# Attention and state update of the sample tokens moved from the MLP's side work into the first state space branch

## The chip, the cores and the metric

The kernel runs on one core of a Trainium2 chip. The metric is the device time of one execution in microseconds (us), as the median of several runs. TensorE (PE in the profile) multiplies matrices into PSUM, VectorE (DVE) and ScalarE (ACT) do elementwise work, GpSimd (POOL) helps them, and SyncE (SP) issues most of the DMAs that move data between HBM and SBUF. Each engine works through its own list of instructions, in the order of the list.

## The reference

One step of a hybrid decoder layer. 2048 prompt tokens and 8 x 8 new tokens (the sample tokens, 8 sequences with a past of 8192 positions) go through one input projection; then, side by side, a dilated attention and a Mamba-2 state space branch; then one output projection, a squared-ReLU MLP of width 4096, and a norm. Everything is float32.

```python
def layer_prompt(h, lw):
    q, k, v, z, xbc, dt_raw = in_proj(h, jnp.arange(s), norm_mix, w_in)
    groups = [dilated_group_prompt(q, k, v, d, w // d) for (w, d) in DILATED_GROUPS]
    att = combine_groups(groups).reshape(b, s, D_ATT).astype(h.dtype)
    ssm, conv_state, ssm_state = ssm_branch(z, xbc, dt_raw, conv_prefix, h0, ...)
    h = out_and_mlp(h, att, ssm, w_out, norm_mlp, w_up, w_down)

def layer_sample(h, cache_k, cache_v, conv_prefix, h0, lw):
    k_ext = jnp.concatenate([cache_k.astype(k.dtype), k], axis=1)
    groups = [dilated_group_sample(q, k_ext, v_ext, d, w // d, n_past) for (w, d) in DILATED_GROUPS]
    att = combine_groups(groups).reshape(b, t, D_ATT).astype(h.dtype)
    ssm, conv_state, ssm_state = ssm_branch(z, xbc, dt_raw, conv_prefix, h0, ...)
    h = out_and_mlp(h, att, ssm, w_out, norm_mlp, w_up, w_down)
```

The two sample parts of this case are the attention of the new tokens over 1280 cached keys and values of each of the 8 sequences (`sample_att`), and their convolution and state update (`sample_ssm`). Their results are first needed by the output projection of the fourth and last tile of tokens.

## The kernel before

The work has three stages. First the input projection, then the prompt attention, in 16 steps of (key group, 512 tokens), with the rest of the input projection (tile `ps_xz`) woven in; then, tile by tile, output projection and MLP. A tile is 512 tokens, so there are four (T = 0 to 3); the sample tokens ride along with tile 3.

The state space branch of a tile (`branch`, with `ssd` for each of its four chunks of 128 tokens, and `merge`, which adds up the attention's parts) must be done before the tile's output projection `out`. The branch of tile 0 has nothing to hide behind but the end of the attention: the loop `for _ in branch(0, ...)` writes it out before `out(0)`. The branches of tiles 1 to 3 are side work of the MLP of the tile before: `work` yields after each small piece, and `tick`, called 64 times in a tile's MLP, draws as many pieces as the table `PLAN` says. In the kernel before, `work` also draws the sample parts: the state update ahead of the branch in the MLP of tile 0, the attention behind the branch in the MLP of tile 1.

Each multiplication in the projections is done three times, on high and low halves of the operands (`mm`, three matmuls of 512 columns a step); the weights are loaded as `raw_m` and split into `wm_h` (ScalarE) and `wm_l` (VectorE). The sample parts multiply float32 as it is, which TensorE does in two passes (the trace shows two matmuls for each one written). `sample_att` goes through pairs of sequences: keys (`kts`) times queries into `ps_ss`, with the mask added into `Sx` on VectorE; maximum, exponential, sum; eleven transposes into `ps_pt`, copied to `PT`; `PT` times values (`vts`) into `ps_po`; and two transposes into `ps_ao`. `sample_ssm` makes a convolution (`cv_s`), then for each of the 8 sequences loads a state `h0`, multiplies into `ps_yos` and `ps_sts` and adds the new state `hn_s`, and ends with a norm (`ps_sss`).

The order on each engine is set by a scheduler, which moves an instruction ahead of others where its own estimate of times says so, and by the pools: a tile that takes the place of an older one waits for the last use of that one. Pools stand on a left and a right stack. A hand-made dependency (`ld`, `behind`) keeps the first loads of the state update behind a certain load of output weights (`k.og`).

Of the kernel before, what the change touches and what calls it, by code (L numbers as in the profile page):

```python
# [9 lines left out]
F32 = mybir.dt.float32  # L10
# [7 lines left out]
P = 128  # L18
# [23 lines left out]
NBC = 2  # L42
# [8 lines left out]
NB2 = BS + max(SM)  # L51
WORK = ('', 'sb', 'ba', 'b')
LEAD = 4
# [11 lines left out]

PLAN = (plan((10, 10), (46, 48)), plan((38, 48), (18, 26)), plan((56, 48)))
OG = 3
# [39 lines left out]
def build(nc, tc, ctx, I, O, dbg=None, stop=None):  # L107
    dbg = dbg or {}
    k = K()
# [48 lines left out]
    pn = K()  # L158
# [672 lines left out]
    atx.close()  # L831
    te0 = p1x.enter_context(tc.tile_pool(name="te0", bufs=1, reuse_waits="tile", side="right"))
    tx0 = p1x.enter_context(tc.tile_pool(name="tx0", bufs=1, reuse_waits="tile", side="right"))
    if stop == "at":
        p1x.close()
        for nm, t in (("o12_s", o12_s), ("o3_s", o3_s), ("den_s", den_s), ("xzs_s", xzs_s)):
            if nm in dbg:
                nc.sync.dma_start(dbg[nm], t)
        return
# [38 lines left out]

    cx = ExitStack()
    tp = cx.enter_context(tc.tile_pool(name="dtp", bufs=1, reuse_waits="tile"))  # L880
    dent = tp.tile([P, P], F32, name="dent")
# [199 lines left out]
    def work(T, mix):  # L1081
        for part in WORK[T]:
            if part == "b":
                yield from branch(T, mix, pn)
            elif part == "s":
                yield from sample_ssm(nc, tc, I, O, psm, ident, ones, E)
            else:
                yield from sample_att(nc, tc, I, O, psm, ident, qs_s, ks_s, smx, kn_s)
        if SM[T]:
            mixsmp(T, mix)  # L1090

    def mm(ps, wh, wl, xh, xl, nk=4, first=True, last=True, after=None):
        for kk in range(nk):
# [7 lines left out]
    E = dict(dtv=dtv, ea_s=ea_s, nacum=nacum, wend=wend, decs=decs, bmask=bmask, convw=convw, convb=convb, dskip=dskip,  # L1101
             normw=normw, half_neg=half_neg, dr=dr, xzs_s=xzs_s, acs_s=acs_s, qs_s=qs_s, ks_s=ks_s, smx=smx, ld=lambda d: behind(d, k.og))
    for _ in branch(0, mix, nc, NBC, tx0, te0):
        pass
    wout0 = [load_wm(I["wout"][0, :, 4 * h:4 * h + 4]) for h in range(2)] if W0 else None
    cx.close()
    p1x.close()
    if stop == "smp":
# [221 lines left out]
def sample_ssm(nc, tc, I, O, psm, ident, ones, E):  # L1330
# [3 lines left out]
    NT = DB * DT  # L1334
    ld = E["ld"]
    with ExitStack() as cx:
        sp = cx.enter_context(tc.tile_pool(name="smp1", bufs=1, reuse_waits="tile"))
        mix = sp.tile([P, 4, NT], F32, name="mix")
# [110 lines left out]
def sample_att(nc, tc, I, O, psm, ident, qs_s, ks_s, smx, kn_s):  # L1449
    NT = DB * DT  # L1450
    with ExitStack() as cx:
        sp = cx.enter_context(tc.tile_pool(name="smp", bufs=1, reuse_waits="tile"))
        mix = sp.tile([P, 4, NT], F32, name="mixA")
# [25 lines left out]
        for bp in range(DB // 2):  # L1479
            Sx = sp.tile([P, NEWP + DT], F32, tag="Sx", name="Sx", bufs=1)  # L1480
            V = []
            for be in range(2):
# [5 lines left out]
                for n0 in range(0, NEWP + DT, 512):  # L1488
# [3 lines left out]
                    for pr in range(2):  # L1492
                        kt = sp.tile([P, 512], F32, tag="kts", name="kts", bufs=3)
                        nc.sync.dma_start(kt[:, :m1 - n0], I["kTs"][b][:, pr, n0:m1])
                        lq = qz[:, pr, b].rearrange("p e j t -> p (e j t)")
                        o = ps[r0 + 32 * pr:r0 + 32 * pr + 32]
                        nc.tensor.matmul(o[:, :m1 - n0], lq, kt[:, :m1 - n0], start=True, stop=True, skip_group_check=True)
                        if n1 > NEWP:
                            nc.tensor.matmul(o[:, m1 - n0:n1 - n0], lq, kn[:, pr, b * DT:(b + 1) * DT], start=True, stop=True,
                                             skip_group_check=True)  # L1500
# [24 lines left out]
            for be in range(2):  # L1525
                o = po[64 * be:64 * be + 64, :256]
                for j in range(5):
                    v = sp.tile([P, 2, 256], F32, tag="vts", name="vts", bufs=2)
                    nc.sync.dma_start(v, I["vTs"][2 * bp + be][:, 2 * j:2 * j + 2])
# [174 lines left out]
```

## Time and profile before

| | us |
|---|---|
| median of 3 runs | 2806.09 |
| lowest, highest | 2802.56, 2806.14 |
| the profiled execution, its own time | 2806.49 |
| its span in the trace | 2804.8 |

The page gives for each engine its busy time: TensorE 2627.4 us (94% of the span), VectorE 1718.9 (61%), ScalarE 1164.7 (42%), GpSimd 487.3 (17%). In the parts of a page and the answers of the trace, L1531 is line 1531 of the kernel, PE matmuls, PEld the weight loads before them; `ps_po<-vts,PT` is what an instruction writes and reads, by tile names. A matmul's record runs from its start until its result is there, over the start of the next one. The granted clock is a share of TensorE's full 2.4 GHz. Idle time of an engine carries the name of what ended it.

### The profile page before, as it was taken

The page shows a single profiled execution, that of the slowest core. Times are in us where ns is not written, and L with a number is a line of the kernel's source. Part 1 is how long each engine was busy: PE and PEld are TensorE (multiplying, and loading weights), DVE is VectorE, ACT ScalarE, POOL GpSimd, SP SyncE. Part 2 cuts the span into 40 slices and gives each one's busy share as a digit, 9 for nine tenths or more (in the row PEclk, how much of TensorE's full clock was granted, in tenths as well). Part 3 has the DMA queues.
Part 4 walks back from the last instruction along what each step waited for, and adds up shares of the span by engine and source line. Part 5 has one row for each costly group of instructions (what it writes and reads, how often), then busy time and mean ns, then how long its engine had stood idle before and what let it go on. Part 6 is the DMA issues. An engine that isn't in the chain of part 4 may idle for free.

```text
span 2804.8 us, 41924 instructions
## 1 busy us (share of the span) xinstructions
PE 2627.4 (94%) x15190; PEld 2274.1 (81%) x15190; DVE 1718.9 (61%) x2995; ACT 1164.7 (42%) x2243; POOL 487.3 (17%) x406
## 2 busy tenths in 40 slices
PE   7999699999854899999999999999999999999998
PEld 7999699899743677888888886666678889999998
DVE  6444277767797745777558775444477764555455
ACT  5333245454563424444454443233255344332333
POOL 2221044534443210010121010011010003000000
PEclk9999899999856899999999999999999999999999
DMA  7666687979344544454465445465455424533332
GB/s 253 205 208 186 176 256 198 262 221 261 115 125 142 182 152 154 147 165 134 153 210 169 148 141 174 135 200 176 156 177 165 152 100 158 174 101 105 104 102 83
DMA packets 341439, 464.30 MB, mean 166 GB/s; under 512 B 38096, under 2 KB 217488, under 8 KB 340192
## 3 DMA queue, kind: packets, MB, share of 16 engines
q1 hardware_dynamic: 314768, 437.96, 50.3%
q10 hardware_dynamic: 26464, 23.66, 2.6%
q8 instruction: 120, 1.97, 0.3%
q14 instruction: 87, 0.71, 0.1%
HBM read 366.12 MB, written 128.96 MB: 177 GB/s over the span
## 4 chain that ended last, share of the span: by engine, by line
PE 84%; DMA 6%; DVE 5%; SPq 2%; issue 2%; ACT 1%; POOL 1%; DVEq 0%; ACTq 0%; POOLq 0%
PE ps_dn L1094 9%; PE ps_dn L1096 9%; PE ps_up L1096 9%; PE ps_up L1094 9%; PE ps_dn L1097 9%; PE ps_up L1097 9%; PE ps_qk L600 3%; PE ps_o L1096 2%; PE ps_o L1094 2%; PE ps_o L1097 2%; PE ps_xz L180 2%; PE ps_xz L183 2%; PE ps_xz L184 2%; PE ps_po L1531 1%; PE ps_pv L724 1%
## 5 line engine op out<-in xcount | busy, mean ns | idle before, releaser
L873 ACT ACTIVATE wm_h<-raw_m 128x512 fp32r<-128x512 f32 x576 | 362.1, 630 | 838.0 <-PE ps_dn L1096 474.4
L874 DVE TENSOR_TENSOR wm_l<-raw_m,wm_h 128x512 fp32r<-128x512 f32 x576 | 416.5, 725 | 121.0 <-ACT wm_h L873 102.3
L1094 PE MATMUL ps_up<-xh_m,wm_h 128*128 128x512 f32 (+1 forms) x1280 | 458.6, 358 | 0.0
L1094 PE MATMUL ps_dn<-uh,wm_h 128*128 128x512 f32 (+1 forms) x1280 | 458.5, 359 | 0.0
L1096 PE MATMUL ps_dn<-ul,wm_h 128*128 128x512 f32 (+1 forms) x1280 | 457.1, 357 | 0.0
L1096 PE MATMUL ps_up<-xl_m,wm_h 128*128 128x512 f32 (+1 forms) x1280 | 456.9, 357 | 0.0
L1097 PE MATMUL ps_dn<-uh,wm_l 128*128 128x512 f32 (+1 forms) x1280 | 456.0, 357 | 0.0
L1097 PE MATMUL ps_up<-xh_m,wm_l 128*128 128x512 f32 (+1 forms) x1280 | 455.7, 356 | 0.0
L1207 DVE TENSOR_TENSOR acc<-acc,ps_dn 128x512 f32<-128x512 f32 (+1 forms) x320 | 189.4, 593 | 241.1 <-PE ps_dn L1097 238.0
L1094 PEld LDWEIGHTS ps_dn<-uh,wm_h 128*128 128x128 f32 x1280 | 240.3, 188 | 43.5 <-issue 11.0
L1096 PEld LDWEIGHTS ps_dn<-ul,wm_h 128*128 128x128 f32 x1280 | 240.3, 188 | 39.0 <-issue 6.5
L1096 PEld LDWEIGHTS ps_up<-xl_m,wm_h 128*128 128x128 f32 x1280 | 241.1, 188 | 37.1 <-issue 4.5
L1097 PEld LDWEIGHTS ps_dn<-uh,wm_l 128*128 128x128 f32 x1280 | 240.5, 188 | 37.6 <-issue 4.1
L1097 PEld LDWEIGHTS ps_up<-xh_m,wm_l 128*128 128x128 f32 x1280 | 241.4, 189 | 35.5 <-issue 2.0
L1094 PEld LDWEIGHTS ps_up<-xh_m,wm_h 128*128 128x128 f32 x1280 | 241.2, 188 | 34.5 <-issue 1.2
L1195 DVE SCALAR_TENSOR_TENSOR r<-ps_up,rs 128x512 f32<-128x512 f32 (+1 forms) x160 | 95.5, 597 | 141.7 <-PE ps_up L1097 140.5
L1198 DVE TENSOR_TENSOR ul<-r,uh 128x512 fp32r<-128x512 f32 (+1 forms) x160 | 96.7, 604 | 93.3 <-ACT uh L1197 93.3
L180 PE MATMUL ps_xz<-xq,wh 128*128 128x256 f32 (+1 forms) x512 | 146.6, 288 | 7.2 <-DMA xq<-xn_s 7.1
L183 PE MATMUL ps_xz<-xq,wh 128*128 128x256 f32 (+1 forms) x512 | 146.6, 287 | 0.0
L184 PE MATMUL ps_xz<-xq,wl 128*128 128x256 f32 (+1 forms) x512 | 145.8, 286 | 0.0
L600 PE MATMUL ps_qk<-qt,kA 128*128 128x256 f32 x300 | 103.5, 355 | 41.1 <-DMA qt<-q_s 35.1
L1196 ACT ACTIVATE r<-r 128x512 f32<-128x512 f32 (+1 forms) x160 | 88.8, 555 | 115.4 <-DVE r L1195 114.6
(355 smaller groups left out, 5273.6 us busy)
## 6 DMA issues: line engine op xcount, KB each, us to landing
raw_m<-wup SPq DMA_DIRECT2D x256, 256.0 KB
raw_m<-wdn SPq DMA_DIRECT2D x256, 256.0 KB
xq<-xn_s SPq DMA_DIRECT2D x48, 512.0 KB
am<-o_s SPq DMA_DIRECT2D x128, 128.0 KB
raw_m<-wout SPq DMA_DIRECT2D x64, 256.0 KB
ks<-ck SPq DMA_DIRECT2D x32, 510.0 KB
vs<-cv SPq DMA_DIRECT2D x32, 510.0 KB
xz_s<-ev SPq DMA_DIRECT2D x96, 128.0 KB
```

The costliest lines, as they stand in the source:

```text
L180: r = nc.tensor.matmul(ps, wh(kk), xh(kk), start=kk == 0, stop=False)
L183: nc.tensor.matmul(ps, wh(kk), xl(kk), start=False, stop=False)
L184: k.zl = nc.tensor.matmul(ps, wl(kk), xh(kk), start=False, stop=kk == KT - 1)
L600: k.mm = nc.tensor.matmul(ov, kt[:, ksl], mv, start=first, stop=False, skip_group_check=True)
L873: k.at["ACT"] = nc.scalar.activation(hi, raw, AF.Copy)
L874: nc.vector.tensor_tensor(lo, raw, hi.bitcast(F32), op=ALU.subtract)
L1094: behind(nc.tensor.matmul(ps, wh[:, kk], xh(kk), start=first and kk == 0, stop=False), after)
L1096: nc.tensor.matmul(ps, wh[:, kk], xl(kk), start=False, stop=False)
L1097: r = nc.tensor.matmul(ps, wl[:, kk], xh(kk), start=False, stop=last and kk == nk - 1)
L1195: nc.vector.scalar_tensor_tensor(r, ps, 0.0, c(X.rs), op0=ALU.max, op1=ALU.mult)
L1198: nc.vector.tensor_tensor(c(ul), r, c(uh).bitcast(F32), op=ALU.subtract)
L1207: k.at["DVE"] = nc.vector.tensor_tensor(h, h, ps, op=ALU.add)
```

## The change

The two sample parts leave `work` and become one generator, `samples()`: attention first, then state update. While the branch of tile 0 is written out, one piece of it is drawn after each piece of the branch, from the fourth on; what is left is drawn behind. `PLAN` becomes the same for three tiles: 48 pieces of a branch over 56 slots. The sample parts take their PSUM banks from the pool `pa` (three banks, as the projections do) instead of `pm`. Their SBUF pools stand on the right stack, in the place of the input projection's weights, whose pool now closes as soon as the attention is written out; the tiles of branch 0 (`te0`, `tx0`) move from the right stack to the left, in the place of the attention's tiles. The key loads get 6 buffers instead of 3, the value loads 4 instead of 2, and the dependency `ld` goes.

```diff
-WORK = ('', 'sb', 'ba', 'b')
+WORK = ('', 'b', 'b', 'b')
...
-PLAN = (plan((10, 10), (46, 48)), plan((38, 48), (18, 26)), plan((56, 48)))
+PLAN = (plan((56, 48)),) * 3
...
     atx.close()
-    te0 = p1x.enter_context(tc.tile_pool(name="te0", bufs=1, reuse_waits="tile", side="right"))
-    tx0 = p1x.enter_context(tc.tile_pool(name="tx0", bufs=1, reuse_waits="tile", side="right"))
+    p1x.close()
...
     cx = ExitStack()
+    te0 = cx.enter_context(tc.tile_pool(name="te0", bufs=1, reuse_waits="tile"))
+    tx0 = cx.enter_context(tc.tile_pool(name="tx0", bufs=1, reuse_waits="tile"))
...
         for part in WORK[T]:
-            if part == "b":
-                yield from branch(T, mix, pn)
-            elif part == "s":
-                yield from sample_ssm(nc, tc, I, O, psm, ident, ones, E)
-            else:
-                yield from sample_att(nc, tc, I, O, psm, ident, qs_s, ks_s, smx, kn_s)
+            yield from branch(T, mix, pn)
...
-    for _ in branch(0, mix, nc, NBC, tx0, te0):
+    def psp(name):
+        return pa.tile([P, 512], F32, tag="pa", name=name)
+
+    def samples():
+        yield from sample_att(nc, tc, I, O, psp, ident, qs_s, ks_s, smx, kn_s)
+        yield from sample_ssm(nc, tc, I, O, psp, ident, ones, E)
+
+    smp = samples()
+    for i, _ in enumerate(branch(0, mix, nc, NBC, tx0, te0)):
+        if i >= LEAD - 1:
+            next(smp, None)
+    for _ in smp:
         pass
     wout0 = [load_wm(I["wout"][0, :, 4 * h:4 * h + 4]) for h in range(2)] if W0 else None
     cx.close()
-    p1x.close()
...
-    ld = E["ld"]
+    ld = lambda d: d
...
-        sp = cx.enter_context(tc.tile_pool(name="smp1", bufs=1, reuse_waits="tile"))
+        sp = cx.enter_context(tc.tile_pool(name="smp1", bufs=1, reuse_waits="tile", side="right"))
...
-        sp = cx.enter_context(tc.tile_pool(name="smp", bufs=1, reuse_waits="tile"))
+        sp = cx.enter_context(tc.tile_pool(name="smp", bufs=1, reuse_waits="tile", side="right"))
...
-                        kt = sp.tile([P, 512], F32, tag="kts", name="kts", bufs=3)
+                        kt = sp.tile([P, 512], F32, tag="kts", name="kts", bufs=6)
...
-                    v = sp.tile([P, 2, 256], F32, tag="vts", name="vts", bufs=2)
+                    v = sp.tile([P, 2, 256], F32, tag="vts", name="vts", bufs=4)
```

What the scheduler makes of it is seen at three places. The first is VectorE's list in the last steps of the prompt attention (`S`, `M`, `den` and `lo` are the attention's tiles; `cv`, `xc` and `zt` are those of branch 0; `Sx` and `mixA` the sample attention's). Before:

```order
L672 TENSOR_TENSOR M<-S_6884,S_6909 128x1024
L930 SCALAR_TENSOR_TENSOR cv<-xc,convw,cv 128x128
L104 TENSOR_TENSOR lo<-S_6718,hi 128x512
L930 SCALAR_TENSOR_TENSOR cv<-xc,convw,cv 128x128 x2
L675 TENSOR_TENSOR M<-M,S_6265 128x2x256
L675 TENSOR_TENSOR M<-M,S_6266 128x2x256
L930 SCALAR_TENSOR_TENSOR cv<-xc,convw,cv 128x128 x8
L104 TENSOR_TENSOR lo<-S_6743,hi 128x512
```

And VectorE now, at the same place:

```order
L672 TENSOR_TENSOR M<-S_6884,S_6909 128x1024
L104 TENSOR_TENSOR lo<-S_6718,hi 128x512
L675 TENSOR_TENSOR M<-M,S_6265 128x2x256
L675 TENSOR_TENSOR M<-M,S_6266 128x2x256
L734 TENSOR_TENSOR den<-S_6265,S_6718 128x2x256
L734 TENSOR_TENSOR den<-S_6266,S_6718 128x2x256
L104 TENSOR_TENSOR lo<-S_6743,hi 128x512
L737 TENSOR_TENSOR den<-den,S_6743 128x1024
L104 TENSOR_TENSOR lo<-S_6743,hi 128x512
L1550 COPY mixA<-ps_ao 64x2x2x8 x4
L1507 TENSOR_TENSOR Sx<-ps_ss,sk 64x512 x2
```

The convolutions of the branch's first two chunks (48 instructions, L930) stood among the attention's and now stand behind all of it; in their place are the first two pairs of the sample attention.

The second place is SP's list where the loads of branch 0 begin (`xc`, `ar`, `zt`, `ea`). Before, among the loads of the last steps of the attention:

```order
L623 DMA V_6711<-v_s 128x4x128
L901 DMA xc<-xz_s 128x8x128
L627 DMA dV_6713<-v_s 128x4x128
L903 DMA ar<-ac_s 128x1024
L908 DMA zt<-xz_s 128x4x128
L912 DMA ea<-ac_s 64x4x128 x2
```

And SP now, behind the attention's last stores (`o_s`):

```order
L1500 DMA kts<-kTs 128x512 x4
L770 DMA o_s<-O_7191 1024x1x128
L884 DMA r_s<-dent 128x128
L1500 DMA kts<-kTs 128x256 x2
L770 DMA o_s<-O_7213 1024x1x128
L1500 DMA kts<-kTs 128x512 x4
L1500 DMA kts<-kTs 128x256 x2
L901 DMA xc<-xz_s 128x8x128
L903 DMA ar<-ac_s 128x1024
L908 DMA zt<-xz_s 128x4x128
```

The first load of the branch has moved behind the attention's end and behind two rounds of key loads, each round of which fills all six key buffers.

The third place is TensorE's list ahead of the first output projection (`ps_o`; `ps_ys` and `ps_sss` are the end of the state update). Before, it stood in the middle of branch 0:

```order
L1003 MATMUL ps_ss<-ones_r,sq_9389 128x1 x2
L947 MATMUL ps_xt<-ident,cv 128x128 x4
L955 MATMUL ps_bt<-ident,cv 128x128
L956 MATMUL ps_bt<-cv 128x128
L955 MATMUL ps_bt<-ident,cv 128x128
L956 MATMUL ps_bt<-cv 128x128
L1094 MATMUL ps_o<-mix_9265,wm_h 128x512
```

And TensorE now:

```order
L1407 MATMUL ps_yos<-h_10446,cm 64x256 x2
L1407 MATMUL ps_yos<-h_10463,cm 64x256 x2
L1426 MATMUL ps_ys<-ident,yo 128x64 x4
L1429 MATMUL ps_ys<-ar_s,xdt_s 64x64 x8
L1442 MATMUL ps_sss<-ones_r,sq_s 64x1 x2
L1089 MATMUL ps_o<-mix_9267,wm_h 128x512
```

The first output projection now stands behind all but the last matmul of the state update.

## Rows read from the trace of the kernel before

**Rows 1.** The page's second part: tenths of busy time and granted clock, 40 slices.

```profile
PE   7999699999854899999999999999999999999998
...
PEclk9999899999856899999999999999999999999999
```

**Rows 2.** Windows: stretch us, its length, busy us (instructions) by engine, clock, DMA share, GB/s.

```profile
core 0: us, PE busy (x) PEld busy (x) DVE busy (x) ACT busy (x) POOL busy (x), PEclk, DMA share, GB/s
735.00:840.00 105.00, 61.33 (x233) 48.09 (x233) 98.58 (x137) 63.83 (x122) 52.67 (x33) 0.61 0.44 126
840.00:934.00 94.00, 43.51 (x202) 31.23 (x201) 63.20 (x137) 32.40 (x72) 25.88 (x21) 0.64 0.39 120
...
1100.00:1690.00 590.00, 590.00 (x2734) 479.34 (x2733) 422.43 (x778) 274.08 (x520) 74.84 (x66) 1.00 0.50 161
1690.00:2060.00 370.00, 370.00 (x1552) 252.64 (x1552) 168.40 (x276) 121.89 (x211) 23.36 (x20) 1.00 0.53 168
2060.00:2600.00 540.00, 540.00 (x3295) 488.89 (x3294) 334.28 (x625) 223.74 (x429) 51.10 (x49) 1.00 0.43 139
```

**Rows 3.** Groups by line, TensorE, 1690 to 2060 us: x count, busy us, mean ns, idle.

```profile
L1531 PE MATMUL ps_po<-vts,PT 128*64 128x256 f32 x160 | 41.8, 390 | 0.0
...
L1497 PE MATMUL ps_ss<-kts,qz 128*32 128x512 f32 (+1 forms) x96 | 35.6, 532 | 0.0
...
L1472 PE MATMUL ps_kn<-ident,kn 128*64 128x128 f32 x2 | 0.4, 270 | 0.0
```

**Rows 4.** Groups by line, TensorE, 970 to 1100 us.

```profile
L1407 PE MATMUL ps_sts<-xw_s,bm 64*128 64x256 f32 x32 | 9.0, 402 | 0.0
L1401 PE MATMUL ps_yos<-h,cm 128*64 128x256 f32 x32 | 8.4, 389 | 0.0
...
L1436 PE MATMUL ps_sss<-ones_r,sq_s 128*64 128x1 f32 x4 | 0.4, 202 | 0.0
```

**Rows 5.** Chain of waits, 1690 to 2060 us, shares by line.

```profile
by line: PE ps_dn L1094 10.9%; PE ps_dn L1096 10.8%; PE ps_up L1096 10.7%; PE ps_po L1531 10.7%; PE ps_up L1097 10.6%; PE ps_up L1094 10.4%; PE ps_dn L1097 10.4%; PE ps_ss L1497 8.7%; PE ps_o L1096 4.3%; PE ps_o L1094 4.2%; PE ps_o L1097 4.
```

**Rows 6.** Groups by line, VectorE, 1690 to 2060 us.

```profile
L874 DVE TENSOR_TENSOR wm_l<-raw_m,wm_h 128x512 fp32r<-128x512 f32 x95 | 66.2, 698 | 42.4 <-ACT wm_h L873 39.0 <-ACT ao L1536 2.1 <-DMA h_s<-hst 1.0
...
L1501 DVE TENSOR_TENSOR Sx<-ps_ss,sk 64x512 f32<-64x512 f32 (+1 forms) x24 | 14.3, 602 | 26.3 <-PE ps_ss L1497 21.2 <-PE ps_ss L1499 5.1
...
L1456 DVE MEMSET qz<- 128x512 f32 x1 | 0.5, 485 | 0.1
```

**Rows 7.** Groups by line, VectorE, 930 to 1100 us.

```profile
L1353 DVE SCALAR_TENSOR_TENSOR cv_s<-xc_s,convw,cv_s 128x64 f32<-128x64 f32 x24 | 6.9, 348 | 0.0
...
L1437 DVE TENSOR_SCALAR rc_p<-ps_sss 64x2 f32<-64x2 f32 x1 | 0.2, 151 | 0.7 <-PE ps_sss L1436 0.7
```

**Rows 8.** Timeline, VectorE: start us, us, line, what, [idle before, releaser].

```profile
786.01 1.16 DVE L930 SCALAR_TENSOR_TENSOR cv<-xc,convw,cv 128x128 f32<-128x128 f32 x1
...
838.92 0.69 DVE L104 TENSOR_TENSOR lo<-S,hi 128x512 fp32r<-128x512 f32 x1 [0.44 <-ACT hi L103]
...
847.15 0.95 DVE L883 RECIPROCAL dent<-dent 128x128 f32<-128x128 f32 x1 [2.59 <-DMA dent<-den_s]
...
923.80 0.16 DVE L1004 TENSOR_SCALAR rc_s<-ps_ss 128x2 f32<-128x2 f32 x1 [3.90 <-PE ps_ss L1003]
...
928.59 0.69 DVE L104 TENSOR_TENSOR mix<-y,mix 128x512 fp32r<-128x512 f32 x1 [0.69 <-ACT mix L103]
...
934.31 0.69 DVE L1150 TENSOR_TENSOR hst<-hst,ps_o 128x512 f32<-128x512 f32 x1 [4.43 <-PE ps_o L1097]
```

**Rows 9.** Groups by line, VectorE, 735 to 934 us.

```profile
L104 DVE TENSOR_TENSOR lo<-S,hi 128x512 fp32r<-128x512 f32 x28 | 23.8, 859 | 5.0 <-ACT hi L103 5.0
```

**Rows 10.** DMA issues by line, 1690 to 2060 us: count, KB each.

```profile
vts<-vTs SPq DMA_DIRECT2D x40, 256.0 KB
...
kts<-kTs SPq DMA_DIRECT2D x32, 256.0 KB
...
kts<-kTs SPq DMA_DIRECT2D x16, 128.0 KB
```

More of the change, by code (lines that the diff above doesn't have):

```diff
@@ L1101, in build @@
     E = dict(dtv=dtv, ea_s=ea_s, nacum=nacum, wend=wend, decs=decs, bmask=bmask, convw=convw, convb=convb, dskip=dskip,
-             normw=normw, half_neg=half_neg, dr=dr, xzs_s=xzs_s, acs_s=acs_s, qs_s=qs_s, ks_s=ks_s, smx=smx, ld=lambda d: behind(d, k.og))
-    for _ in branch(0, mix, nc, NBC, tx0, te0):
+             normw=normw, half_neg=half_neg, dr=dr, xzs_s=xzs_s, acs_s=acs_s, qs_s=qs_s, ks_s=ks_s, smx=smx)
+    def psp(name):
[8 more added lines that the diff above has]
+    for _ in smp:
         pass
@@ L1106, in build @@
     cx.close()
-    p1x.close()
     if stop == "smp":
```

## The prediction

> **What bounds the kernel now.** I read the page's slices first: TensorE is at nine tenths from the fifteenth slice to the end, and dips before it, down to 4 and 5, where the granted clock dips too [rows 1]. The windows by stage say how deep. From 1100 to 2600 us TensorE is busy in every microsecond, at clock 1.00, whether sample work is there (1690 to 2060) or not (2060 to 2600) [rows 2]. So in the MLP a microsecond of TensorE is one of the program. From 735 to 934 us it is otherwise: TensorE is busy 61.33 + 43.51 = 104.8 of 199 us at a clock of 0.61 and 0.64, and VectorE 98.58 + 63.20 = 161.8. VectorE has hardly a gap in the first part, the attention's end (6.4 of 105 us), and 30.8 of 94 in the second, branch 0 alone [rows 2]. The timeline shows why: the convolutions of the branch start at 786, among the attention's work; the attention's last split is at 838.9; then VectorE waits in short steps for a store to come back (dent, 2.59 us) and for a chain through TensorE and GpSimd (rc_s, 3.90 us), until the last `mix` at 928.6 lets the first full output projection end at 934.3 [rows 8]. I call 735 to 934.3 us the stretch; VectorE bounds it first, the branch's chain second.
>
> **What leaves the MLP.** Sample attention on TensorE, seven groups from L1531 (160 matmuls, 41.8 us) and L1497 (96, 35.6 us) to L1472 (0.4 us), sums to 92.6 us [rows 3]. The state update, nine groups from L1407 (9.0) and L1401 (8.4) to L1436 (0.4), sums to 22.0 [rows 4]. These are lengths of records, which run over the start of the next. The chain gives L1531 and L1497 10.7% and 8.7% of 370 us, 71.8 us [rows 5], where the groups say 77.4: a factor 0.928. So (92.6 + 22.0) x 0.928 = 106 us of a full engine go. Nothing I see is late in their place: without sample work TensorE was still busy 540 of 540 us [rows 2]. The other side work of the MLP, three branches, stays.
>
> **What the stretch takes on.** VectorE: sample attention, seven groups from 14.3 (L1501) to 0.5 us (L1456), together 31.6 [rows 6]; state update, 19 groups from 6.9 (L1353) to 0.2 (L1437), together 25.7 [rows 7]. Sum 57.3, call it 58 with a few more weight splits that now stand ahead of the first `hst`. VectorE's list keeps all its other work, only in another order: before the attention's last split it loses two chunks of convolutions and gets two pairs of sequences, behind it the reverse and the rest. If VectorE's idle time stays as long as it was (37 us), the stretch grows by 58.
>
> Three things speak for more. First, branch 0 starts late: its first load stands behind two rounds of key loads, and the second round needs its six buffers back, that is, TensorE's products of the first round. While SP waits there, everything behind is late too: the branch's loads, the merge's, and the next values. Where VectorE before had convolved chunks to go on with, it has a few Sx rows. Second, the first part will hardly shrink by the convolutions it loses, since sample matmuls now sit between the attention's on TensorE and wait for keys. Third, the first output projection stands behind the end of the state update, a chain VectorE - TensorE - VectorE - ScalarE - VectorE - TensorE; before, 5.7 us lay between the last `mix` and the first `hst` [rows 8]. No row shows these waits. From below they are worth less than nothing: the sample work may fill gaps of VectorE, at most all 37 us [rows 2]. From above I bound them by the stretch's own worst: if each part had as much idle time again as the second part (30.8 us), +62. I take +15, near the 13 us that the two waits of 2.59 and 3.90 us make if each comes twice [rows 8]: about 7 for the first part, 8 for the ends of the second. So the stretch grows by 58 + 15 = 73.
>
> The other engines have room, if only just. DMA: 40 x 256 KB of values and 32 x 256 + 16 x 128 KB of keys are 20 MB [rows 10]; the stretch moved 126 and 120 GB/s at a share of 0.44 and 0.39 [rows 2], so about 290 GB/s at a full share, and 20 MB are some 70 us of the 115 us that are free in 199. The loads cost nothing in sum, though in the first part more than half of them meet the attention's own. TensorE: 106 us more at full clock beside 104.8 x 0.62 = 65 us makes 171 of 272.
>
> **Two rules against the change.** The same form of split, two SBUF inputs of 128x512, took 859 ns in the stretch [rows 9] and 698 in the MLP [rows 6], and GpSimd is busy 52.67 of 105 us there against 23.36 of 370 [rows 2]. The Trainium skill, GPSIMD Engine Reference, Specifications, says that GpSimd's way to SBUF is shared with VectorE and that the two contend when a VectorE instruction has two SBUF inputs; the trace agrees in kind. By that rule, and with the whole ratio of 1.23, the 58 us would be 71 and the time 13 us longer; I leave it in the range, since most sample instructions have one input in PSUM or one input alone.
>
> The other is the clock, and gives a rival: granted 1.00 where TensorE is always busy, 0.61 where it is busy for 58% [rows 2], which is a mix of its levels of 1.2 and 2.4 GHz. The Trainium skill, TensorE: Matmul & The Clock Gate, What's actually happening, says that the throttled state is the default and only activity releases it; the trace agrees. So the moved matmuls are dearer where they go unless they themselves keep the clock up.
>
> **The sum.** Against the profiled execution: 2806.5 - 106 + 73 = 2773.5, say 2774 us. Its own time is 0.4 us over the median of 2806.09, which changes nothing.
>
> **Rivals.**
> - *The gaps fill.* Sample pieces and branch pieces do not depend on each other, so one's waits are the other's work. For it: 30.8 us of idle time in branch 0 that come from one chain with nothing beside it [rows 2, 8]. Against it: lists are in order, and a sample instruction that waits for keys holds the branch. With half the 37 us filled, the stretch grows by 58 - 18 = 40: 2740 us.
> - *TensorE becomes the bound of the stretch (slower).* If the clock stays low, because TensorE keeps waiting for keys, values, splits and upper masks in turn, 106 us become 212 at 1.2 GHz; with the 104.8 us that are there, 317 us instead of 199, a growth of 118: 2806.5 - 106 + 118 = 2818. For it: the clock of 0.61 with matmuls spread over the whole stretch, and attention matmuls that now queue behind sample ones that wait for a load. Against it: slices next to the dip with TensorE at nine tenths have the full clock [rows 1]. It decides the sign once the stretch grows by more than 106.
> - *The MLP does not give it all back.* If the splits of weights (L874, 66.2 us in 370 [rows 6]) or their loads cannot follow a TensorE freed of side work, part of the 106 is lost; with a fifth lost, 2795. Against it: the 540 us without sample work [rows 2].
>
> **How the numbers follow.** Forecast 0.60, with 2756 to 2798 as its own range; gaps fill 0.17; TensorE bound 0.16; MLP keeps a part 0.07. A measurement of this kernel can tell about 0.2%, 5.6 us, from no change: faster means below 2800.5. The forecast is faster but for 0.03, the second all of it, of the third 0.13 slower and 0.03 the same, of the last half faster. So faster 0.77, same 0.09, slower 0.14. The range, 2738 to 2812, reaches to the gap-filling time, with GpSimd's contention and most of TensorE's rival at the other end.
>
> **What would show it.** In the profile after: no `ps_po`, `ps_sts` in the MLP, TensorE still without a gap there, and the MLP from the first `hst` to the end shorter by some 106 us; the first `hst` near 934 + 73 = 1007 us; the attention's last split between 838 and 850; VectorE busy about 220 us between 735 and that `hst`; the clock in the stretch well over 0.62. The prediction is wrong in the MLP if TensorE shows idle time there, and wrong in the stretch if the first `hst` is before 970 or behind 1040 us.

## The result, and the profile after

The changed kernel took 2770.36 us (median of 4 runs, 2763.89 to 2775.28), the kernel before, beside it on the same chip, 2804.32. The ratio is 0.988, with a 95% interval of 0.9855 to 0.9904: 1.2% faster. The prediction was 2774 us, with 2738 to 2812 as its range. The profiled execution after is the fastest of the four, 2763.89 us with a span of 2762.2.

The page's second part after, tenths of busy time of TensorE and its granted clock in 40 slices, which answers to [rows 1]:

```profile
PE   7999789999986689999999999999999999999998
...
PEclk9999889999998789999999999999999999999999
```

The dip is still there, two slices wide, but not so deep: 6 and 6 where it was 5 and 4, and the clock falls to 7 instead of 5. The windows of the changed kernel, with the columns of [rows 2]:

```profile
735.00:840.00 105.00, 90.21 (x440) 59.22 (x439) 89.78 (x123) 56.08 (x99) 48.62 (x31) 0.90 0.72 224
840.00:1009.50 169.50, 107.69 (x461) 65.71 (x461) 120.47 (x289) 59.41 (x140) 36.23 (x32) 0.75 0.60 172
1100.00:1690.00 590.00, 590.00 (x2689) 478.96 (x2688) 389.88 (x702) 258.11 (x479) 60.99 (x54) 1.00 0.49 155
1690.00:2060.00 370.00, 370.00 (x1676) 300.37 (x1675) 234.32 (x420) 164.69 (x301) 42.55 (x36) 1.00 0.50 158
2060.00:2560.00 500.00, 500.00 (x3111) 457.04 (x3110) 291.71 (x534) 199.31 (x377) 42.93 (x43) 1.00 0.41 132
```

In the MLP TensorE is again busy in every microsecond at clock 1.00, now without sample work. In the first part of the stretch it has gone from 61 to 90 us of 105, and the clock from 0.61 to 0.90: the moved matmuls keep it up themselves. VectorE's timeline of the changed kernel (start, length, line, what, idle before and its releaser), which answers to [rows 8]:

```profile
835.62 0.69 DVE L104 TENSOR_TENSOR lo<-S,hi 128x512 fp32r<-128x512 f32 x1 [1.57 <-ACT hi L103]
...
843.16 0.69 DVE L1507 TENSOR_TENSOR Sx<-ps_ss,sk 64x512 f32<-64x512 f32 x1 [3.30 <-PE ps_ss L1503]
...
855.18 5.50 DVE L930 SCALAR_TENSOR_TENSOR cv<-xc,convw,cv 128x128 f32<-128x128 f32 x17 [3.00 <-ACT cv L928]
...
983.54 0.69 DVE L104 TENSOR_TENSOR mix<-y,mix 128x512 fp32r<-128x512 f32 x1
...
998.16 0.86 DVE L1433 SCALAR_TENSOR_TENSOR y_s<-cv_s,dskip,ps_ys 128x64 f32<-128x64 f32 x4 [3.12 <-PE ps_ys L1429]
...
1006.42 0.69 DVE L872 TENSOR_TENSOR wm_l<-raw_m,wm_h 128x512 fp32r<-128x512 f32 x1 [5.27 <-ACT wm_h L871]
1008.72 0.86 DVE L1450 SCALAR_TENSOR_TENSOR mix<-y_s,normw,ps_sss 128x64 f32<-128x64 f32 x4 [1.61 <-PE ps_sss L1447]
1009.49 0.68 DVE L1156 TENSOR_TENSOR hst<-hst,ps_o 128x512 f32<-128x512 f32 x1
```

The attention's last split is at 835.6 us (838.9 before). The first convolutions come at 855.2 instead of 786.0. The branch's last `mix` is at 983.5, and the first `hst`, 5.7 us behind the branch before, now follows 26 us later, behind the state update's end (L1433, L1450). So the stretch ends at 1009.5 us instead of 934.3: it grew by 75.2 us. From there to the end the program takes 2762.2 - 1009.5 = 1752.7 us instead of 2804.8 - 934.3 = 1870.5: 117.8 less. The balance is 42.6 us, which is the difference of the two spans. By the medians, 2804.32 and 2770.36, the change is worth 34.0 us.

### The profile page after: what moved, and what is told of

Same layout as the page of the kernel before. It is cut to its first block, busy times and chain, and to the rows that moved or that the text cites. A ratio compares the mean times of both kernels' runs of the same rounds, so it can differ in the third digit from the quotient of the medians.

```text
span 2762.2 us, 41935 instructions
## 1 busy us (share of the span) xinstructions
PE 2602.3 (94%) x15190; PEld 2279.2 (83%) x15190; DVE 1701.0 (62%) x2995; ACT 1165.7 (42%) x2243; POOL 480.1 (17%) x406
## 4 chain that ended last, share of the span: by engine, by line
PE 73%; DMA 4%; DVE 2%; ACT 1%; issue 1%; SPq 0%; POOL 0%; DVEq 0%; ACTq 0%; POOLq 0%
PE ps_dn L1089 9%; PE ps_up L1089 9%; PE ps_dn L1091 9%; PE ps_up L1091 9%; PE ps_dn L1092 9%; PE ps_up L1092 9%; PE ps_o L1091 2%; PE ps_o L1089 2%; PE ps_o L1092 2%; PE ps_qk L600 2%; PE ps_pv L724 1%; PE ps_xz L180 1%; PE ps_xz L183 1%; PE ps_xz L184 1%; PE ps_po L1537 1%; DMA xq<-xn_s 1%
## 5 line engine op out<-in xcount | busy, mean ns | idle before, releaser
L99 POOL TENSOR_TENSOR y<-y,zt 128x512 f32<-128x512 f32 x12 | 15.5, 1296 | 806.1 <-DVE y L99 415.9
```

## The experiments

All times are the median of four runs or more, beside runs of the kernel before on the same chip, with the interval of the ratio to it. "Projection" is the first `hst`, and "the rest" what lies behind it, both from the profiled execution. I give for each kernel what each theory expected, then what came. The three kernels of the last experiment leave the stretch as the changed kernel has it, and their first `hst` came at 1010.0, 1010.0 and 1015.9 us, against 1009.5; so up to some 6 us between two single profiled executions are no finding.

**What the stretch and the MLP take without sample work.** Both sample parts left out:

```
-    yield from sample_att(nc, tc, I, O, psp, ident, qs_s, ks_s, smx, kn_s)
-    yield from sample_ssm(nc, tc, I, O, psp, ident, ones, E)
+    zero = c2.tile([P, DB * DT], F32, name="zero")
+    nc.vector.memset(zero, 0.0)
+    for t in smx:
+        for kt in range(KT):
+            nc.scalar.activation(t[:, kt, :], zero, AF.Copy)
+    yield
```

> The changed kernel with sample attention and sample state update left out altogether (the sample tokens' mixture is set to zero). It tells what the stretch and the MLP take with no sample work anywhere. The theory (the growth of 75 us is VectorE's work of the samples, 49 us, and 26 us of waits among sample instructions, and nothing else): the first full output projection at 930 to 940 us as before the change, the MLP behind it 1753 us long as in the changed kernel, so about 2690 us in all. The rival (part of the growth is the later start of branch 0, whose tiles now lie where the attention's were): the projection at 950 to 965 us, 2705 to 2720 us.

It took 2697.97 us (ratio 0.9612, 0.9594 to 0.9629). The first `hst` in VectorE's timeline:

```profile
940.90 0.69 DVE L1160 TENSOR_TENSOR hst<-hst,ps_o 128x512 f32<-128x512 f32 x1 [2.42 <-PE ps_o L1092]
```

That is 6.6 us behind the kernel before, though its first convolutions come at 833.9 us, 48 us later than before. The rest is 1752.6 us, the same as in the changed kernel to 0.1 us. So a start that is 48 us late costs little, 6.6 of 75.2 us, about what two executions can differ by; the rival that gave it 15 to 30 us fell, and the theory's 930 to 940 was passed by a microsecond. In the changed kernel the branch starts 69 us late; no run shows what the 21 us more cost by themselves. The other 68.6 us come with the sample work, and in the MLP all of the 117.9 us do.

**Each half alone.** First attention alone, with the state update left in the MLP of tile 0:

```
-WORK = ('', 'b', 'b', 'b')
-PLAN = (plan((56, 48)),) * 3
+WORK = ('', 'sb', 'b', 'b')
+PLAN = (plan((10, 10), (46, 48)), plan((56, 48)), plan((56, 48)))
...
 def samples():
     yield from sample_att(nc, tc, I, O, psp, ident, qs_s, ks_s, smx, kn_s)
-    yield from sample_ssm(nc, tc, I, O, psp, ident, ones, E)
...
```

> Half of the change: sample attention moves to the stretch, the state update stays in the MLP of tile 0 with its old plan. With no sample work anywhere the first full output projection came at 940.9 us and 1752.6 us lay behind it. The theory (each part costs the stretch in proportion to its VectorE work, 31.6 of 57.3 us, and the MLP in proportion to its TensorE work, 92.6 of 114.6 us, of the 68.6 and 117.9 us measured for both; the tail of the state update in front of the first projection is gone): projection at 979 to 986 us, 1775 us behind it, 2756 to 2763 us in all, so 0.3 to 0.5% below the changed kernel. The rival (attention brings nearly all of the growth, since its keys, products and softmax form the long chains): projection at 995 to 1005 us, 2772 to 2782 us.

It took 2755.24 us (0.9822, 0.9806 to 0.9838), an interval wholly below that of the changed kernel. The branch's last `mix` and the first `hst` in its timeline:

```profile
975.60 0.69 DVE L104 TENSOR_TENSOR mix<-y,mix 128x512 fp32r<-128x512 f32 x1 [0.69 <-ACT mix L103]
...
981.44 0.69 DVE L1158 TENSOR_TENSOR hst<-hst,ps_o 128x512 f32<-128x512 f32 x1 [4.55 <-PE ps_o L1095]
```

Projection at 981.4 us, the rest 1774.9: both as the theory had them. There are 5.8 us between the two rows, as before the change, where the changed kernel has 26. Then the state update alone, with attention left in the MLP of tile 1 (`WORK` with 'ba' for tile 1, the old plan and buffers):

> The other half: the state update moves to the stretch, sample attention stays in the MLP of tile 1 with its old plan and buffers. The theory (as for the first half): projection at 965 to 972 us (940.9 + 24 to 31), 1752.5 + 95 = 1848 us behind it, 2814 to 2821 us in all, slower than the kernel before by 0.3 to 0.5%, since the state update brings more to the stretch than it takes from the MLP (23 us). The rival (attention brings nearly all of the growth): projection at 945 to 953 us, 2794 to 2802 us.

2828.92 us (1.0089, 1.007 to 1.0109). Its first `hst`:

```profile
972.61 0.69 DVE L1158 TENSOR_TENSOR hst<-hst,ps_o 128x512 f32<-128x512 f32 x1 [3.35 <-PE ps_o L1095]
```

Behind it lie 1850.0 us. Projection and rest are the theory's, one and two microseconds above its upper ends; the median lies 8 us above its range. So, in profiled executions (the MLP always against the kernel before):

| moved | stretch grows by | MLP shrinks by |
|---|---|---|
| nothing (sample work left out) | 6.6 | 117.9 |
| attention alone, over that | 40.5 | 95.6 (1870.5 - 1774.9) |
| state update on top of attention | 28.1 | 22.2 (1774.9 - 1752.7) |
| state update alone, over the first row | 31.7 | 20.5 (1870.5 - 1850.0) |

All of the gain is attention's. The state update costs the stretch more than it takes from the MLP, in either setting, and the medians say the same: 2770.36 us with both parts moved, 2755.24 with attention alone, 2828.92 with the state update alone.

**Which engine bounds the stretch.** Each product of sample queries and keys issued twice, in the kernel before and in the changed one:

```
 nc.tensor.matmul(o[:, :m1 - n0], lq, kt[:, :m1 - n0], start=True, stop=True, skip_group_check=True)
+nc.tensor.matmul(o[:, :m1 - n0], lq, kt[:, :m1 - n0], start=True, stop=True, skip_group_check=True)
```

> The kernel before, with each of the 48 products of sample queries and keys (`ps_ss` from `kts`) issued twice into the same place; the result is the same. There the products stand in the MLP of tile 1. The theory (TensorE is the bound of the MLP, a microsecond of it is one of the program): the chain gave these products 8.7% of 370 us, their group 35.6 us, so the time grows by 32 to 36 us over the kernel before. The rival (the MLP has slack elsewhere, so that side work is partly free): under 20 us.

> The changed kernel with the same 48 products issued twice; now they stand in the stretch. The theory (VectorE and waits bound the stretch, TensorE has room there): the first full output projection comes 0 to 12 us later than the 1009.5 us of the changed kernel, and the time grows by as much. The rival (TensorE has become the bound of the stretch): the same 32 to 36 us as in the MLP at full clock, up to 64 us at 1.2 GHz.

In the kernel before it cost 23.8 us by the medians (1.008, 1.006 to 1.01), and 22.2 us in the rest of the profiled execution: between the two expectations. A second copy in the same burst thus costs 22.2 us, or 231 ns for each of its 96 records, and not the 32 to 36 us of the first (31.0 us from step to step in the kernel before); what the first has on top is looked for below. In the changed kernel, at 2785.18 us (0.9931, 0.9914 to 0.9947), the theory failed, and the rival's 32 us did not come either. The first `hst`, and the window up to the attention's last split (at 858.3 instead of 835.6):

```profile
1028.96 0.68 DVE L1156 TENSOR_TENSOR hst<-hst,ps_o 128x512 f32<-128x512 f32 x1
```

```profile
735.00:858.00 123.00, 109.61 (x527) 66.68 (x526) 93.38 (x128) 57.74 (x101) 46.66 (x31) 0.92 0.66 201
```

The projection is 19.5 us late, nearly the 22.2 that the same products cost in the MLP. TensorE is busy 109.6 of 123 us there and VectorE 93.4: in the first part TensorE now has the less room of the two. The counterpart puts an addition that nobody reads behind each `Sx` on VectorE:

```
 nc.vector.tensor_tensor(Sx[r0:r0 + 64, n0:n1], ps[r0:r0 + 64, :n1 - n0], sk[r0:r0 + 64, n0:n1], op=ALU.add)
+junk = sp.tile([P, 512], F32, tag="junk", name="junk", bufs=1)
+nc.vector.tensor_tensor(junk, sk[:, :512], sk[:, 512:1024], op=ALU.add)
```

> The changed kernel with one more VectorE addition (128x512, two inputs in SBUF, into a tile that nothing reads) behind each of the 24 `Sx` additions: 24 x 0.70 to 0.86 = 17 to 21 us of VectorE's time that nobody waits for. The theory (VectorE bounds the stretch): the first full output projection and the end come 12 to 21 us later. The rival (waits bound it, VectorE has room): 0 to 6 us. A result between the two would say that the stretch has a bound that changes from piece to piece.

2782.8 us (0.9918, 0.99 to 0.9936), as the theory had it, the projection 15.1 us late for 17.1 us more of VectorE's busy time (the 24 additions take 23.1 us, 962 ns each, and the stretch's other instructions got shorter):

```profile
1024.56 0.68 DVE L1156 TENSOR_TENSOR hst<-hst,ps_o 128x512 f32<-128x512 f32 x1
```

So both engines pass on most of what is added to them, and neither alone is the bound. That fits pieces that go from one to the other in turn (product, `Sx`, transpose, product), though no run here takes that chain apart. By the medians the two kernels are 14.8 and 12.4 us over the changed one, a little less.

**Loads.** Keys and values loaded for the first sequence only, and used for all:

```
-kt = sp.tile([P, 512], F32, tag="kts", name="kts", bufs=6)
-nc.sync.dma_start(kt[:, :m1 - n0], I["kTs"][b][:, pr, n0:m1])
+if b == 0:
+    kt = sp.tile([P, 512], F32, name=f"kts{n0}_{pr}")
+    nc.sync.dma_start(kt[:, :m1 - n0], I["kTs"][b][:, pr, n0:m1])
+    KEEP[n0, pr] = kt
+kt = KEEP[n0, pr]
...
```

> The changed kernel with keys and values of the sample attention loaded for the first sequence only and used for all eight (7 of 8 of these loads are left out, the results of the other sequences are not the reference's). VectorE, ScalarE and TensorE do the same work. The theory of the prediction (part of the growth is waits for keys, since each round of loads needs its buffers back from TensorE, and SP stands there with the branch's loads behind it): of the 21 us of waits a half or more goes, projection at 985 to 1000 us, 2745 to 2760 us. The rival (the waits come from the chains between engines, not from loads): projection at 1005 to 1010 us, 2765 to 2772 us.

2755.56 us (0.9825, 0.9811 to 0.984), with 14.8 us off the projection:

```profile
989.74 0.69 DVE L104 TENSOR_TENSOR mix<-y,mix 128x512 fp32r<-128x512 f32 x1 [0.69 <-ACT mix L103]
...
994.65 0.69 DVE L1156 TENSOR_TENSOR hst<-hst,ps_o 128x512 f32<-128x512 f32 x1 [3.02 <-PE ps_o L1092]
```

The loads do cost the stretch that much. The rows show where: the branch's last `mix` comes 6.2 us later than in the changed kernel, but the state update is done before it, and only 4.9 us instead of 26 lie between that `mix` and the first `hst`. Whether it is for want of buffers was tried with attention alone, which leaves room for 12 key and 10 value buffers:

```
-tag="kts", name="kts", bufs=6
+tag="kts", name="kts", bufs=12
-tag="vts", name="vts", bufs=4
+tag="vts", name="vts", bufs=10
```

> Sample attention alone moved, as before, with 12 buffers for keys and 10 for values instead of 6 and 4, which the place freed by the state update allows. With the loads left out for 7 of 8 sequences the projection came 14.8 us earlier. The theory (those 15 us are loads that wait for a buffer to come back): 5 to 12 us earlier than with 6 and 4, projection at 969 to 976 us, 2743 to 2750 us in all. The rival (they are the transfers themselves beside the attention's own, or the place comes free later for so large a pool): within 3 us of 2755, or slower.

2758.52 us (0.9841, 0.9824 to 0.9858), projection at 983.0 instead of 981.4: no gain. With attention alone it is not the number of buffers; with the state update behind it, where the 15 us were found, no run tries it. What in the loads costs them (the transfers beside the attention's own, or SP's order) stays open.

**State update first.** The two parts in the other order:

```
-yield from sample_att(...)
-yield from sample_ssm(...)
+yield from sample_ssm(...)
+yield from sample_att(...)
```

> The changed kernel with the two sample parts in the other order: state update first, attention behind it. In the changed kernel the branch's last `mix` is at 983.5 us and the first output projection's matmuls start only at 1000.9, behind the state update's last chain. The theory (that tail is a cost of order, about 15 us, and attention's last chain is shorter): projection at 995 to 1004 us, 2756 to 2766 us. The rival (what stands last costs the same, whichever part it is, or the state update in the first part costs as much there as it saves at the end): projection at 1006 to 1016 us, 2767 to 2777 us.

2793.05 us (0.9957, 0.9942 to 0.9971): projection at 1042.6, worse than both expectations. VectorE's longest waits there, 735 to 1042 us (line waited for, us in total, times, longest):

```profile
DVE mixA L1550 <- PE ps_ao L1545: 24.7, 3, 13.3
DVE hn_s L1418 <- PE ps_sts L1413: 9.6, 1, 9.6
DVE cv L930 <- ACT cv L928: 8.4, 3, 6.0
```

Two waits grew. Among the attention's end, an addition of the state update (`hn_s`) that waited for its product held VectorE's list for 9.6 us, and the attention's last split came at 861.7 instead of 835.6. At the end the last sequences' way through TensorE and ScalarE to `mixA` stood alone: 34 us between the branch's last `mix` (1008.6) and the first `hst`, against 26 in the changed kernel. So the state update is the worse neighbour of the attention's end, and attention the longer tail.

**The edge of a burst.** In the kernel before, the steps from one matmul's start to the next's say that an MLP matmul beside a sample matmul took longer than among its own kind. The sample matmuls take float32, the MLP's fp32r; most sample matmuls also use a part of TensorE's array (the rows say `128*64`, `128*32` or `64*128`), the MLP's all of it (`128*128`). Three kernels put matmuls of their own in front of `ps_dn` groups; the first:

```
+raw = pl.tile([P, 512], F32, tag=tg, name="ps_dn")
+ps = c.bank(raw)
+nc.tensor.matmul(raw[:64, :128], ident[:, :64], ident, start=True, stop=True, skip_group_check=True)
```

> The changed kernel with one float32 matmul (identity, 128x128, 64 rows out) in front of each of the 320 groups of `ps_dn` matmuls in the MLP, written into the place that the group then overwrites: 320 bursts of one. The theory (a float32 matmul among the MLP's fp32r ones costs its own time and an edge of about 0.18 us a burst, because in the trace of the kernel before an MLP matmul next to a sample matmul took 312 to 335 ns and one among its own kind 233): own time at most 320 x 0.27 = 86 us by the record of that form, edges 320 x 0.18 = 58 us, about 145 us over the changed kernel. The rival (no edge; the long steps were waits of the sample work): 86 us or less, the same as with bursts of four.

> The same 320 float32 matmuls in 80 bursts of four, in front of every fourth group. The theory: the same own time, but only 80 edges, 80 x 0.18 = 14 us, so about 100 us over the changed kernel and 43 us less than with bursts of one. The rival (no edge): within 8 us of the bursts of one.

> The control: at the same 320 places one more fp32r matmul of the group's own operands (128x512, overwritten by the group), so a burst without a change of type. The theory (the edge comes with the change between fp32r and float32): 320 x 0.233 = 75 us over the changed kernel (less in tile 3, whose groups are narrower: 256 x 0.233 + 64 x about 0.14 = 69), nothing on top. The rival (any matmul more at these places breaks the stream and pays an edge): 69 + 58 = 127 us.

Measured: bursts of one 2946.03 us (ratio 1.0517, 1.0501 to 1.0532), bursts of four 2862.98 (1.0223, 1.0206 to 1.0239), fp32r 2829.17 (1.01, 1.0083 to 1.0116). In the rest of the profiled executions that is 175.7, 97.2 and 61.3 us over the changed kernel's 1752.7. TensorE's timeline with bursts of one (the third row is one float32 matmul of `128*64`, two records):

```profile
1502.42 0.40 PE L1091 MATMUL ps_dn<-ul,wm_h 128*128 128x512 f32 x1
1502.65 0.40 PE L1092 MATMUL ps_dn<-uh,wm_l 128*128 128x512 f32 x1
1502.98 0.43 PE L1212 MATMUL ps_dn<-ident 128*64 128x128 f32 x2
1503.34 0.50 PE L1089 MATMUL ps_dn<-uh,wm_h 128*128 128x512 f32 x1
1503.68 0.40 PE L1091 MATMUL ps_dn<-ul,wm_h 128*128 128x512 f32 x1
1503.91 0.40 PE L1092 MATMUL ps_dn<-uh,wm_l 128*128 128x512 f32 x1
```

and with fp32r:

```profile
1303.06 0.40 PE L1092 MATMUL ps_dn<-uh,wm_l 128*128 128x512 f32 x1
1303.29 0.40 PE L1212 MATMUL ps_dn<-uh,wm_h 128*128 128x512 f32 x1
1303.53 0.40 PE L1089 MATMUL ps_dn<-uh,wm_h 128*128 128x512 f32 x1
```

The start is what counts here, since a record runs over the start of the next. Among themselves the MLP's matmuls start every 0.23 us. The last one before the float32 matmul takes 0.33, the float32 one 0.36, and the first behind it 0.34. The fp32r one fits in at 0.23 on both sides. Over all bursts the means are 326 and 338 ns for the two neighbours (233 among their own kind), and 160 + 202 for the two float32 records, which take 109 each inside a burst of four. So an edge costs 93 + 105 + 51 + 93 = 342 ns a burst. With 315 bursts (some had merged in the list) and 636 records that makes 315 x 0.342 + 636 x 0.109 = 177 us, measured 175.7; with 89 bursts and 640 records 100, measured 97.2; the fp32r matmuls, 192 x 0.233 + 128 x 0.132 = 61.6, measured 61.3. The theory had half the size of an edge; that it came out near for bursts of four, 100 us, is luck (86 us of own time against 70, 14 of edges against 30). The control excludes that just any matmul more breaks the stream. But the theory's cause, the change of type, is not it. The control differs from the first kernel in type, in shape on the array and in width at once, and the branches, which stay in the MLP, tell these apart: their matmuls are float32 as well, and some take all of the array. TensorE in the changed kernel, at such a place:

```profile
1171.06 0.39 PE L1092 MATMUL ps_up<-xh_m,wm_l 128*128 128x512 f32 x1
1171.29 0.59 PE L1008 MATMUL ps_ss<-dg_s,ones_r 128*128 128x256 f32 x2
1171.53 0.58 PE L1089 MATMUL ps_up<-xh_m,wm_h 128*128 128x512 f32 x1
1171.95 0.39 PE L1091 MATMUL ps_up<-xl_m,wm_h 128*128 128x512 f32 x1
```

From the first of these starts to the last are 0.89 us. That is two MLP matmuls (2 x 0.233) and two float32 records at the 0.216 us that one of this size takes inside a longer burst (`ps_st`): nothing is left for an edge, in the mean of the 12 such bursts either (0.896 us). The bursts that begin with `ps_xt` (128x128) and with L1003 (128x1), both of the whole array, show none either. In front of the 12 `ps_y` bursts (float32, `128*64`), on the other hand, the last MLP matmul takes 0.326 us. So the edge goes with the shape on the array and not with the type.

## Why the prediction came out right

**What leaves the MLP: 106 forecast, 117.8 measured.** Step to step, the sample matmuls themselves took 105.6 us in the kernel before, so the factor of 0.928 on the groups [rows 3 to 5] was right. The missing 12 us are the MLP's own matmuls that stood beside them: their steps summed to 1686.6 us before and 1674.3 after. The trace has 152 bursts of side work in the MLP before and 74 after (the branches' stay), and the last experiment shows what an edge does to the neighbours; an estimate from it, 78 bursts x (93 + 105) ns, is 15 us. The term was right, and one was left out. That nothing is late in their place was right: TensorE has no gap there, and the rest was 1752.4 to 1753.5 us in five kernels whatever their stretch was (1755.4 in the one with most loads left out).

**What the stretch takes on: 73 forecast, 75.2 measured,** but not by the parts named. I had 58 us of VectorE and 15 of waits. VectorE's busy time grew by 48.5 us (161.8 to 210.2) and its idle time by 26.7 (37.5 to 64.2). That the sum fits is luck: 9.5 us too much work and 11.7 too little waiting cancel. The sample instructions were not cheaper than said. The groups of the changed kernel from 735 to 1009 us, two of them:

```profile
L104 DVE TENSOR_TENSOR lo<-S,hi 128x512 fp32r<-128x512 f32 x28 | 20.8, 755 | 9.0 <-ACT hi L103 8.9
...
L1507 DVE TENSOR_TENSOR Sx<-ps_ss,sk 64x512 f32<-64x512 f32 (+1 forms) x24 | 14.3, 601 | 10.8 <-PE ps_ss L1503 8.3 <-PE ps_ss L1505 2.3
```

`Sx` has its 14.3 us as in [rows 6], and the records of all sample instructions, which overlap a little, sum to 63 us. What fell are the stretch's own, from 178.4 to 166.2 us: the 28 `lo` take 755 ns instead of 859 [rows 9]. The prediction kept the rule on GpSimd's way to SBUF as a possible 13 us more. The rows point the other way: with about the same GpSimd work (busy 78.6 us before, 84.9 after) fewer instructions were held up beside it, 8 of the 96 convolutions instead of 12 and 4 of the 28 `lo` instead of 5. What these two groups take beyond their length without GpSimd (341 and 685 ns) fell from 14 to 7 us, over half of the 12; the last heading tells how. No run was made for it.

The waits, by parts: up to the attention's last split, from there to the branch's last `mix`, and from there to the first `hst`. Before:

```profile
735.00:838.92 103.92, 60.59 (x229) 47.52 (x228) 97.88 (x136) 62.89 (x121) 52.67 (x33) 0.61 0.44 125
838.92:928.59 89.67, 38.85 (x194) 27.82 (x192) 62.60 (x136) 31.30 (x71) 25.88 (x21) 0.65 0.42 127
928.59:934.31 5.72, 5.70 (x13) 4.24 (x14) 1.29 (x2) 2.05 (x4) 0.00 (x0) 0.53 0.13 46
```

And after:

```profile
735.00:835.62 100.62, 85.83 (x412) 56.89 (x411) 85.75 (x114) 54.02 (x96) 48.62 (x31) 0.90 0.70 219
835.62:983.54 147.92, 95.72 (x422) 56.37 (x420) 115.29 (x277) 57.18 (x135) 33.06 (x29) 0.77 0.65 183
983.54:1009.49 25.95, 16.34 (x69) 11.66 (x69) 9.20 (x20) 4.28 (x9) 3.17 (x3) 0.67 0.41 134
```

VectorE's idle time, the length less its busy time, grew from 6.0 to 14.9 us in the first part, where I had put 7; from 27.1 to 32.6 in the second, where I had nothing; and from 4.4 to 16.8 in the tail, where I had 8. In the kernel without sample work the second part has 33.0 too, so its growth fits the late start of the branch. The three reasons given were there, then, and under-priced; the third was the largest. Two signs were missed by a little: the attention's last split came at 835.6 and not between 838 and 850, and VectorE was busy 210 and not 220 us.

The tail is what grew most, and nothing in the computation asks for it. The sample tokens lie in tile 3 alone (`SM`), so tile 0's projection doesn't need the state update; it only stands behind it in TensorE's list. What the tail costs is not shown, though. The state update alone leaves no such tail (5.8 us between the two rows) and still costs the stretch 31.7 us. The loads, which I had as nothing in sum, cost 14.8 us by the kernel with most of them left out.

**The rivals.** *TensorE becomes the bound* did not come at its price: the clock did not stay low, 0.90 and 0.75 against 0.61 and 0.64 [rows 2]. The Trainium skill, TensorE: Matmul & The Clock Gate, What's actually happening, says that the throttled state is the default and activity releases it; the trace agrees, since the same place with TensorE busier got the higher clock. But its first half was true, and that VectorE bounds the stretch first does not hold for the changed kernel: doubled key products were passed on to 19.5 of 22.2 us. The room of 101 us that I counted for TensorE (272 - 171) is there in sum only. *The gaps fill* was wrong: VectorE's idle time rose. *The MLP keeps a part* was wrong by the five equal rests.

The forecast of 2774 was thus 3.6 us off the median because two misses, 12 us too little from the MLP and 2 too little in the stretch, stand against the profiled execution's being 6.5 us under its own median. What leaves the MLP was well founded; that the total came so close is luck.

## What to carry to other kernels

Price each half of a move by itself: here attention paid 96 us for 41, and the state update 22 us for 28, so moving half beats moving all. Side work that takes a part of the array, among a dense stream of matmuls that take all of it, costs an edge per burst besides its own time, so count bursts as well as matmuls. And look at what stands last in front of a stage: a chain that the stage doesn't need can stand ahead of it in a list. Test what it costs before pricing it; here that stayed open.

## What the runs showed of the hardware

A burst of float32 matmuls of `128*64` among fp32r ones of `128*128` costs 342 ns beyond its matmuls at the full clock. A burst of `128*128` costs nothing beyond them, whether fp32r (the control) or float32 (`ps_ss`, L1008).

A VectorE instruction with two inputs in SBUF and one of GpSimd can hold each other up, and then one waits for the other's instruction and does not merely run slower. In the kernel before, VectorE's timeline has these convolutions beside GpSimd's work, which follows in the second fence:

```profile
790.32 1.16 DVE L930 SCALAR_TENSOR_TENSOR cv<-xc,convw,cv 128x128 f32<-128x128 f32 x1
...
794.07 1.39 DVE L930 SCALAR_TENSOR_TENSOR cv<-xc,convw,cv 128x128 f32<-128x128 f32 x5
```

```profile
789.81 1.61 POOL L711 TENSOR_SCALAR_AFFINE_SELECT lou<-lo 128x512 fp32r<-128x512 f32 x1
791.38 0.74 POOL L711 TENSOR_SCALAR_AFFINE_SELECT hiu<-hi 128x512 fp32r<-128x512 f32 x1
792.11 3.22 POOL L676 PARTITION_ALL_REDUCE M<-M  x1
```

The first took 1.16 us and ended 0.06 us behind GpSimd's instruction; the five later ones took 0.34 us each although GpSimd was at work. After the change, VectorE and then GpSimd:

```profile
856.88 1.17 DVE L930 SCALAR_TENSOR_TENSOR cv<-xc,convw,cv 128x128 f32<-128x128 f32 x1
...
898.40 2.71 DVE L930 SCALAR_TENSOR_TENSOR cv<-xc,convw,cv 128x128 f32<-128x128 f32 x10
```

```profile
856.79 1.13 POOL L925 TENSOR_SCALAR_AFFINE_SELECT ar<-ar 128x1024 f32<-128x1024 f32 x1 [35.42 <-DMA ar<-ac_s]
...
898.63 3.43 POOL L925 TENSOR_SCALAR_AFFINE_SELECT ar<-ar 128x1024 f32<-128x1024 f32 x1 [2.51 <-DMA ar<-ac_s]
```

In the first pair the convolution waited; in the second, ten convolutions ran at their usual pace, and GpSimd's `ar`, 1.13 us in the first pair, took 3.43. Of the 96 convolutions of the stretch before, 84 took 327 to 351 ns and 12 took 805 to 1975; 11 of these 12 ended 55 to 149 ns behind the end of a GpSimd instruction (after: all 8 of 592 to 1355 ns, by 140 to 153). The Trainium skill, GPSIMD Engine Reference, Specifications, names this contention for VectorE instructions with two SBUF inputs, without a size; the trace agrees. I had spread the ratio of the two means, 1.23, over all instructions; in truth most pay nothing, and a few pay up to the length of what they wait for.
